# Stick-breaking attention pipelined over head pairs, and a pooling mixer with a root for its first tile alone

## The chip, the cores and the metric

The kernel runs on one core of one Trainium2 chip. The metric is the device time of one execution in microseconds (us), lower is better. Engines are named as the profile names them: PE is the matrix engine (TensorE), DVE is VectorE, ACT is ScalarE, POOL is GpSimd, SP is the engine whose queue issues most transfers. Every engine takes its instructions in the order in which they stand in its own queue and waits at the first one that isn't ready.

## The reference

A trunk of two layers over 512 tokens and 16 meta tokens (528 columns), width 1024. Each layer adds a token mixer and then a SwiGLU network to the residual h. Layer 0 mixes by causal pooling over four window lengths, layer 1 by stick-breaking attention with 16 heads of 64.

```python
def pool_mixer(h, w, scale):          # h is normalised with rmsnorm before
    ...
        outs.append((cs - lag) / cnt - xg)          # window mean minus the token, per group of 256
    pooled = jnp.stack(outs, axis=2).astype(h.dtype)
    mixed = jnp.einsum('blgc,gcd->blgd', pooled, w).reshape(B, L, D_MODEL)
    return mixed * scale

def _sb_attend(qs, qpos, kvs, kpos):
    ...
    z = jnp.einsum('bqhd,bkhd->bhqk', q, k).astype(jnp.float32) * (HEAD_DIM ** -0.5)
    log_keep = jnp.where(mask, jax.nn.log_sigmoid(-z), 0.0)
    later = lax.cumsum(log_keep, axis=3, reverse=True) - log_keep
    a = jnp.where(mask, jnp.exp(jax.nn.log_sigmoid(z) + later), 0.0)
    return jnp.einsum('bhqk,bkhd->bqhd', a.astype(v.dtype), v)
```

After the attention come `@ w_o`, the second SwiGLU network and a last rmsnorm.

## The kernel before

The residual is held transposed, as eight tiles `h0` to `h7` of 128 channels by 528 tokens. Every product is done as three products of a high and a low part: `wsplit` (L82) turns a loaded weight tile into `whi` on ACT (L92) and `wlo` on DVE (L97), and `mm3` (L102) issues the three matmuls per 128 rows (L106). A full weight tile of 1024 columns gives two such splits; the text calls one of them a W.

The order in which instructions stand in each engine's queue is set by a scheduler when the program is built, from the order of the code, from the buffers that are free and from explicit edges (`tc.issue_after(x)`: what the block holds stands behind x on x's engine). On the chip that order is fixed.

Start. Four token tiles x0 to x3 and the meta tile are loaded, their sums of squares are taken (ACT and DVE), `rstd_of` makes the inverse root (one ACT operation and three small DVE ones) for the tiles 0, 4 (meta) and 1 together and then for 2 and 3, and each tile is scaled and split into `ah` (ACT, L224) and `al` (DVE, L225). 30 matmuls on a zero tile (`warm`) run meanwhile. Pooling is a product with a band matrix, first for the left half of the 528 columns over all eight chunks, then for the right half. The mixing product (`mix`, L106, then the DVE addition L265) also runs over all chunks of the left half before the right one; `norm.chunk(c)` (L147) then makes the next network's operands `f0uh`, `f0ul` and the running sum of squares `f0sq` for chunk c.

Attention. The heads come in eight pairs. For a pair p, `proj(p)` has five steps: q (24 matmuls of 512 columns), and each half of k and of v (24 matmuls of 264 columns each). `scores` makes z in three groups of two PSUM banks each (832, 0, 416), and ACT takes two sigmoids of each group, into `kp` and `sg`. `weights(hd)` is, for each of the two heads, a scan over `kp` on DVE (L576) and a product into `sg` (L578). `turned(p, hd)` transposes `sg` on PE into two PSUM tiles `t1` and `t2` (ten transposes and one of `am`, ACT copies of sg's meta columns), which ACT copies into `a1`, `a2` (high parts) and DVE subtracts (low parts, L611) and corrects (`a0`, L614). `attend(p, hd)` multiplies by the values (`po`, nine matmuls), and `finish` splits the pair's output (`os`). `values` transposes v into `pv` and splits it into `vv`. `wo(p0, p1)` is the output product for the pairs p0 to p1-1, in eight steps, one for each chunk of h.

In iteration p of the loop the scores of pair p are issued first, then its values and steps of `proj(p + 1)` as filling, then `turned`, `attend` for both heads. The PSUM tag "two" (z, t1, pv) has two buffers of two banks, the tag "one" (pj, t2, po, pw) four of one bank.

Of the kernel before, what the change touches and what calls it, by code (L numbers as in the profile page):

```python
# [35 lines left out]
WARM = 30  # L36
# [14 lines left out]
def trunk(ctx: ExitStack, tc: tile.TileContext, x, meta, x_t, gain, pool_w, w_qkv, w_o, w_gate, w_up, w_down,  # L51
# [50 lines left out]
    def mm3(outs, wh, wl, xh, xl, start, stop, more=False):  # L102

        for i, (w, xx) in enumerate(((wh, xh), (wh, xl), (wl, xh))):
            for o, sl in outs:
                nc.tensor.matmul(o, lhsT=w, rhs=xx[:, sl], start=start and i == 0, stop=stop and i == 2,  # L106
                                 skip_group_check=more)
# [34 lines left out]


# [35 lines left out]
    with tc.tile_pool(name="start", bufs=1) as sp, phase("ps0", one=8):  # L179
# [11 lines left out]
        nc.sync.dma_start(out=band_raw, in_=c_band)  # L191
        nc.sync.dma_start(out=mband, in_=c_mband)
# [14 lines left out]
        for part in ((0, 4, 1), (2, 3)):  # L207
            i0 = part[0]
            n = len(part)
            ss = sp.tile([P, 3], F32, name=f"ss{i0}")[:, :n]  # L210
            nc.vector.memset(ss, 1.0)
            for j, i in enumerate(part):
                src, acc = (mt, ss[:META, j:j + 1]) if i == 4 else (xt[i], ss[:, j:j + 1])
                if i in (0, 2):
                    nc.scalar.activation(junk[0], src, AF.Square, accum_out=acc)
                else:
                    nc.vector.scalar_tensor_tensor(junk[1][:src.shape[0]], src, 1.0, src, op0=ALU.mult, op1=ALU.mult,
                                                   accum_out=acc)
            nc.vector.tensor_scalar(ss, ss, D * EPS, None, op0=ALU.add)
            r = rstd_of([(ss, slice(0, n))], *[sp.tile([P, 3], F32, name=f"rx{i0}{k}")[:, :n] for k in "rt"])  # L220
            for j, i in enumerate(part):
                rx[i] = r[:, j:j + 1]
        for i in range(4):
            nc.scalar.activation(ah[i], xt[i], AF.Copy, scale=rx[i])  # L224
            nc.vector.scalar_tensor_tensor(al[i], xt[i], rx[i], f32(ah[i]), op0=ALU.mult, op1=ALU.subtract)  # L225
            if i == 1:
                nc.scalar.activation(am[:META], mt, AF.Copy, scale=rx[4][:META])
        nc.vector.tensor_copy(band[:, :, BOFF:BOFF + 144], band_raw)
# [11 lines left out]
        for hf, terms in enumerate((((0, -META), (1, -144)), ((1, 120), (2, HALF - 272), (3, -136)))):  # L240
            for c in range(KC):
                g = c // 2
                cs = slice(c * P, (c + 1) * P)
                pp = ps(f"pool{c}{hf}", "one")[:, :HALF]
                for j, (i, off) in enumerate(terms):
                    rhs = band[:, g, BOFF + off:BOFF + off + HALF]
                    nc.tensor.matmul(pp, lhsT=ah[i][:, cs], rhs=rhs, start=j == 0, stop=False)
                    nc.tensor.matmul(pp, lhsT=al[i][:, cs], rhs=rhs, start=False, stop=j == len(terms) - 1)
                    if hf == 0 and j == 0:
                        nc.tensor.matmul(pp[:, 0:32], lhsT=am[:, cs], rhs=mband[:, g, :], start=False, stop=False)  # L250
                gc = gains[:, c:c + 1]
                a, b = ph[c][:, HV[hf]], pl[c][:, HV[hf]]
                nc.scalar.activation(a, pp, AF.Copy, scale=gc)
                nc.vector.scalar_tensor_tensor(b, pp, gc, f32(a), op0=ALU.mult, op1=ALU.subtract)
        pws = [wsplit(pwr[k], f"pw{k}") for k in range(2)]
        for hf in range(2):
            for c in range(KC):
                g, d = c // 2, c % 2
                pm = ps(f"mix{c}{hf}", "one")[:, :HALF]
                for k in range(2):  # L260
                    ds = slice(d * P, (d + 1) * P)
                    mm3([(pm, HV[hf])], pws[k][0][g][:, ds], pws[k][1][g][:, ds], ph[2 * g + k], pl[2 * g + k],
                        k == 0, k == 1)
                hv = hT[c][:, HV[hf]]
                nc.vector.scalar_tensor_tensor(hv, pm, gains[:, 32 + c:33 + c], hv, op0=ALU.mult, op1=ALU.add)  # L265
                if hf:
                    norm.chunk(c)


    def ffn(layer, gcol, norm, after):  # L270
# [67 lines left out]
        with tc.tile_pool(name=f"ffn{layer}", bufs=1) as fp:  # L338
# [13 lines left out]
            def plain(f):  # L352
                parts = [wsplit(raw_gu(kind, f), f"w{kind}{f}") for kind in ("gate", "up")]
# [131 lines left out]
    with tc.tile_pool(name="att", bufs=1) as ap, phase("ps2", one=4, two=2):  # L485
# [12 lines left out]
        def proj(p):  # L498

            got = {}  # L500
            first = {}

            def half(i, hf):
                if hf == 0:
                    got["w"] = wsplit(wraw(w_qkv[i * KC + p], f"r{'qkv'[i]}{p}"), f"w{'qkv'[i]}{p}")
                    got[i] = blk(f"qf{p}_{i}")
                wh, wl = got["w"]
# [3 lines left out]
                if p == 0:  # L511
                    if hf == 0:
                        first[i] = ps(f"pj{p}_{i}", "two", 2)
                    pj = first[i][:, hf, :n]
                else:
                    pj = ps(f"pj{p}_{i}{hf}", "one")[:, :n]
                for k in range(KC):
                    mm3([(pj, sl)], wh[k], wl[k], uh[k], ul[k], k == 0, k == KC - 1)
# [6 lines left out]
                if i == 0 or (i == 1 and hf == 1):  # L525
                    got["qk"[i]] = parts_of(p, i, f[:, TOK] if i == 0 else f)

# [23 lines left out]
        def scores(p, q, k):  # L551


            (qh, ql), (kh, kl) = q, k
            sg, kp = (ap.tile([P, 2, STRIP], F32, tag=t, name=f"{t}{p}", bufs=1) for t in ("sg", "kp"))

            for o, n, regs in ((832, 512, ((3, 0, META, L),)), (0, 416, ((0, 0, 0, 144), (1, 144, 0, 272))),
                               (416, 416, ((2, 0, 0, 400), (3, 400, 0, META)))):
                tz = ps(f"z{p}_{o}", "two", 2)
# [7 lines left out]
                for d in DIAG:  # L567
                    if o <= d < o + n:
                        for hd in range(2):
                            nc.tensor.matmul(tz[:, hd, d - o:d - o + P], lhsT=masks[:, 2], rhs=masks[:, 0], start=False,  # L570
                                             stop=True, skip_group_check=True)
                for dst, sc in ((kp, -1.0), (sg, 1.0)):
                    nc.scalar.activation(dst[:, :, o:o + n], tz[:, :, 0:n], AF.Sigmoid, scale=sc)  # L573

            def weights(hd):
# [5 lines left out]
            with tc.issue_after(weights(0)):  # L581
                weights(1)
            return sg[:, 0], sg[:, 1]
# [52 lines left out]
        def finish(p, of):  # L636
            a, b = (ap.tile([P, SEQ], F32R, tag="os", name=f"os{p}{n}", bufs=11) for n in "hl")
# [4 lines left out]
        def wo(p0, p1):  # L642
# [4 lines left out]
            def step(c):  # L647
# [5 lines left out]
                for j in range(n):  # L653
                    mm3([(pj, slice(0, SEQ))], wh[j], wl[j], *osp[p0 + j], j == 0, j == n - 1)
                nc.vector.tensor_tensor(out=hT[c][:, TOK], in0=pj, in1=hT[c][:, TOK], op=ALU.add)

            return [lambda c=c: step(c) for c in range(KC)]

        NP = NH // 2
        got, steps, values = proj(0)  # L660
        for st in steps:
            st()
        early = wo(0, 2)
        for p in range(NP):
            of = ap.tile([P, SEQ], F32, tag="of", name=f"of{p}", bufs=1)
            extra = []
            if p < NP - 1:
                nxt, nsteps, nvalues = proj(p + 1)
                before = []
                fill = nsteps[0:1], nsteps[1:2], nsteps[2:3], nsteps[3:4], nsteps[4:]  # L670
                if p == NP - 2:
                    late, fill = nsteps[3:], fill[:3] + ([], [])
                if 3 <= p < NP - 1:
                    extra = early[:4] if p == NP - 2 else early[:2 if p == 3 else 1]
                    early = early[len(extra):]
            else:
                w = wo(2, 4)
                before, fill = late, (w[0:1], w[1:2], w[2:3], w[3:4], w[4:5])
            with tc.issue_after(last) if p else nullcontext():
                s0, s1 = scores(p, got["q"], got["k"])  # L680
            for st in before:
                st()
            values()
            for st in list(fill[0]) + list(fill[1]):
                st()
            w0 = turned(p, 0, s0)
            for st in fill[2]:
                st()
            attend(p, 0, w0, got["v"], of)
            w1 = turned(p, 1, s1)  # L690
            for st in fill[3]:
                st()
            last = attend(p, 1, w1, got["v"], of)
            finish(p, of)
            for st in list(fill[4]) + list(extra):
                st()
            got, values = nxt, nvalues
# [83 lines left out]
```

## Time and profile before

| | us |
|---|---|
| median of 3 runs (lowest, highest) | 1086.45 (1085.02, 1087.53) |
| the profiled execution's own time | 1087.54 |
| its span in the profile | 1085.6 |
| PE busy | 1030.8 (95%) |
| DVE busy | 856.2 (79%) |
| ACT busy | 558.2 (51%) |

The stages, by the first matmuls in the trace: the start until 40.6, the first SwiGLU network until 410.4, attention with its output product until 723.4, the second network and the last norm until the end. A share of the span is a mean over these stages. An instruction's duration is longer than the distance to the next one on the same engine, since neighbours overlap: a matmul of 264 columns is shown as 0.28 and the next one starts 0.12 later. Sums are therefore made from starts.

### The profile page before, as it was taken

To read this page: it belongs to the slowest core of one execution; us is meant where nothing else is said; L and a number is where in the kernel's file an instruction comes from. 1 tells how busy PE (TensorE), PEld (TensorE's weight loads), DVE (VectorE), ACT (ScalarE), POOL (GpSimd) and SP (SyncE) were. 2 spreads that over 40 slices of the span, in tenths; PEclk is the share of its full clock that TensorE was granted. 3 is DMA by queue.
4 is the path that set the end of the run, shared out by engine and by line. 5 is a ranking of instruction groups with operands and counts; after the bars stand their busy time and mean duration, and the time that the engine had idled before them with its cause. 6 is when DMAs were issued, how large, how long until landed. Compare 5 with 4: busy or idle time off the path is not lost.

```text
span 1085.6 us, 18620 instructions
## 1 busy us (share of the span) xinstructions
PE 1030.8 (95%) x7302; PEld 956.6 (88%) x7302; DVE 856.2 (79%) x1529; ACT 558.2 (51%) x1131; POOL 6.2 (1%) x16
## 2 busy tenths in 40 slices
PE   8998999999999999798888899799999999999997
PEld 6997999999999998787788778678899999999985
DVE  7899987878888685766688768789987777878855
ACT  7555644545444454555554545356664454455544
POOL 1000000000000010000000000000000000000000
PEclk9999999999999999899999999899999999999999
DMA  9112332233232332101110102222233232333312
GB/s 346 65 53 73 133 98 98 98 98 98 98 97 98 117 108 88 39 30 40 49 59 21 49 30 79 78 97 69 77 105 101 98 98 97 108 107 117 98 39 78
DMA packets 43111, 95.72 MB, mean 88 GB/s; under 512 B 3328, under 2 KB 20096, under 8 KB 43024
## 3 DMA queue, kind: packets, MB, share of 16 engines
q1 hardware_dynamic: 42272, 93.40, 25.9%
q8 instruction: 57, 0.93, 0.3%
q10 hardware_dynamic: 752, 1.14, 0.3%
q14 instruction: 30, 0.25, 0.1%
HBM read 92.43 MB, written 2.10 MB: 87 GB/s over the span
## 4 chain that ended last, share of the span: by engine, by line
PE 80%; DVE 15%; ACT 2%; issue 1%; DMA 1%; SPq 0%; ACTq 0%; DVEq 0%
PE pb L106 15%; PE pd L106 11%; PE pd L330 11%; PE pj L106 11%; PE pa L106 10%; PE pc L106 10%; DVE kp L576 3%; PE pw L106 2%; PE po L628 2%; PE pp L106 2%; PE z L564 2%; PE t L589 2%; DVE sg L578 1%; DVE xl L389 1%; ACT kp L573 1%
## 5 line engine op out<-in xcount | busy, mean ns | idle before, releaser
L576 DVE TENSOR_TENSOR_SCAN kp<-kp,estrip 128x1344 f32<-128x1344 f32 x16 | 47.3, 2954 | 21.0 <-ACT kp L573 21.0
L303 DVE TENSOR_TENSOR h<-pd,h 128x264 f32<-128x264 f32 x96 | 41.2, 431 | 13.9 <-PE pd L106 13.9
L92 ACT CAST ws_3h<-rgate 128x512 fp32r<-128x512 f32 x38 | 23.6, 621 | 55.3 <-PE pb L106 49.3
L589 PE MATMUL t<-consts,sg 128*128 128x128 f32 x160 | 26.1, 319 | 25.5 <-DVE sg L578 22.4
L92 ACT CAST ws_5h<-s 128x512 fp32r<-128x512 f32 x38 | 23.6, 621 | 47.0 <-PE pb L106 36.3
L589 PEld LDWEIGHTS t<-consts,sg 128*128 128x128 f32 x160 | 21.7, 163 | 28.1 <-issue 24.2
L106 PE MATMUL pa<-xl,ws_0h 128*128 128x264 f32 (+1 forms) x152 | 43.4, 285 | 3.2 <-DVE xl L389 3.2
L432 DVE TENSOR_TENSOR u<-pb,m 128x264 f32<-128x264 f32 (+1 forms) x38 | 16.3, 430 | 38.1 <-PE pb L106 38.0
L92 ACT CAST ws_4h<-s 128x512 fp32r<-128x512 f32 x38 | 23.6, 621 | 42.3 <-PE pa L106 25.6
L106 PE MATMUL pb<-xl,ws_1h 128*128 128x264 f32 (+1 forms) x152 | 43.1, 284 | 1.0 <-DVE xl L389 1.0
L106 PE MATMUL pc<-xh,ws_2l 128*128 128x264 f32 (+1 forms) x152 | 43.2, 284 | 0.0
L106 PE MATMUL pb<-xh,ws_1h 128*128 128x264 f32 (+1 forms) x152 | 43.2, 285 | 0.0
L106 PE MATMUL pa<-xh,ws_3h 128*128 128x264 f32 (+1 forms) x152 | 43.1, 284 | 0.0
L106 PE MATMUL pa<-xh,ws_0l 128*128 128x264 f32 (+1 forms) x152 | 43.1, 284 | 0.0
L106 PE MATMUL pb<-xh,ws_6l 128*128 128x264 f32 (+1 forms) x152 | 43.1, 283 | 0.0
L106 PE MATMUL pa<-xl,ws_3h 128*128 128x264 f32 (+1 forms) x152 | 43.0, 283 | 0.0
L106 PE MATMUL pb<-xh,ws_4l 128*128 128x264 f32 (+1 forms) x152 | 43.0, 283 | 0.0
L106 PE MATMUL pc<-xl,ws_2h 128*128 128x264 f32 (+1 forms) x152 | 43.0, 283 | 0.0
L106 PE MATMUL pc<-xl,ws_5h 128*128 128x264 f32 (+1 forms) x152 | 43.0, 283 | 0.0
L106 PE MATMUL pb<-xl,ws_6h 128*128 128x264 f32 (+1 forms) x152 | 43.0, 283 | 0.0
L106 PE MATMUL pc<-xh,ws_2h 128*128 128x264 f32 (+1 forms) x152 | 43.0, 283 | 0.0
L106 PE MATMUL pb<-xl,ws_4h 128*128 128x264 f32 (+1 forms) x152 | 43.0, 283 | 0.0
(1179 smaller groups left out, 4177.6 us busy)
## 6 DMA issues: line engine op xcount, KB each, us to landing
rgate<-in_ffn_w_gate_dram SPq DMA_DIRECT2D x44, 512.0 KB, 3.5
rup<-in_ffn_w_up_dram SPq DMA_DIRECT2D x44, 512.0 KB, 3.4
rd<-in_ffn_w_down_dram SPq DMA_DIRECT2D x42, 512.0 KB, 3.6
rq<-in_sb_w_qkv_dram SPq DMA_DIRECT2D x8, 512.0 KB, 3.4
rk<-in_sb_w_qkv_dram SPq DMA_DIRECT2D x8, 512.0 KB, 3.4
rv<-in_sb_w_qkv_dram SPq DMA_DIRECT2D x8, 512.0 KB, 3.5
h<-in_x_t_dram SPq DMA_DIRECT2D x8, 264.0 KB, 6.8
x<-in_x_dram SPq DMA_DIRECT2D x4, 512.0 KB, 5.4
```

Source lines behind the costliest of these rows:

```text
L92: nc.scalar.copy(hi, v[:, j:j + w])
L106: nc.tensor.matmul(o, lhsT=w, rhs=xx[:, sl], start=start and i == 0, stop=stop and i == 2, skip_group_check=more)
L303: nc.vector.tensor_tensor(out=hv, in0=pd, in1=hv, op=ALU.add)
L330: nc.tensor.matmul(pd, lhsT=hid[j][x_][:, ts], rhs=w_[:, sl], start=r > 0 and i + j == 0, stop=j == len(hid) - 1 and i == 2, skip_group_ch ...
L389: nc.vector.tensor_tensor(out=xl[i][:, m, :], in0=o, in1=f32(xh[i][:, m, :]), op=ALU.subtract)
L432: tt(out=u[:, a], in0=pb, in1=m1, op=ALU.add)
L564: nc.tensor.matmul(tz[:, hd, c:c + k1 - k0], lhsT=qq[hs, i * P:(i + 1) * P], rhs=kk[hs, k0:k1], start=j == 0 and c == 0, stop=False, skip_ ...
L573: nc.scalar.activation(dst[:, :, o:o + n], tz[:, :, 0:n], AF.Sigmoid, scale=sc)
L576: nc.vector.tensor_tensor_scan(kp[:, hd, ::-1], kp[:, hd, ::-1], estrip[:, ::-1], 1.0, op0=ALU.mult, op1=ALU.max)
L578: return nc.vector.tensor_tensor(out=sg[:, hd, 0:STRIP - 1], in0=sg[:, hd, 0:STRIP - 1], in1=kp[:, hd, 1:STRIP], op=ALU.mult).ins
L589: nc.tensor.transpose(o, sg[:, c0:c0 + n], ident)
L628: last = nc.tensor.matmul(po[:, i0 * P:512], lhsT=lw, rhs=a, start=t == 0 and j == 0, stop=t == 4)
```

## The change

Start: x0 is loaded in two halves on the queues of SP and ACT; the band matrices are loaded on ACT's queue; x0's square is taken by ACT and DVE, half each, and `roots` makes its inverse root alone, then one for tile 1 and meta, then one for 2 and 3. The order of ACT and DVE there is written by hand (`tc.manual_schedule`), with the copy of the band matrix ahead of the first root on DVE. 18 `warm` matmuls instead of 30. Pooling of the left half issues tile 0's products for all chunks first. The mixing product runs chunk by chunk, both halves of a chunk, and `norm.chunk(c)` follows each chunk. The splits of `pool_w` are queued behind the last `split`, those of the first gate and up weights behind chunk 5's pooled halves (`norm.after`).

Attention: `scores` becomes a class with one call for each group, and `begin` issues the three groups of the next pair with steps of `proj` between them, inside the iteration of the pair before: after `turned(p, 1)` and ahead of `attend(p, 1)`. A pair's steps are spread over two iterations (k, k, q in the one, both halves of v in the next). The output product's steps are grouped 0 to 1, 2 to 4 and 5 to 7 instead of 0 to 1, 2 to 3 and 4 to 7: the first group's eight steps are issued in the iterations 4 and 5, the second's in 6 and 7, the third's at the end. `os` has 10 buffers instead of 11.

```diff
-WARM = 30
+WARM = 18
...
-        nc.sync.dma_start(out=xt[0], in_=x[0, 0:P, :])
         nc.scalar.dma_start(out=mt, in_=meta)
+        for h, q in zip(HD2, (nc.sync, nc.scalar)):
+            q.dma_start(out=xt[0][:, h], in_=x[0, 0:P, h])
         nc.sync.dma_start(out=xt[1], in_=x[0, P:2 * P, :])
+        nc.scalar.dma_start(out=band_raw, in_=c_band)
+        nc.scalar.dma_start(out=mband, in_=c_mband)
         nc.scalar.dma_start(out=gains, in_=gain)
...
+        for a in (ah, al):
             for c in range(KC):
+                pool(c, pps[c], 0, -META, (a,), start=a is ah)
...
-        for hf in range(2):
-            for c in range(KC):
-                g, d = c // 2, c % 2
+        for c in range(KC):
+            g, d = c // 2, c % 2
+            for hf in range(2):
                 pm = ps(f"mix{c}{hf}", "one")[:, :HALF]
...
-                if hf:
-                    norm.chunk(c)
+            norm.chunk(c)
...
-            a, b = (ap.tile([P, SEQ], F32R, tag="os", name=f"os{p}{n}", bufs=11) for n in "hl")
+            a, b = (ap.tile([P, SEQ], F32R, tag="os", name=f"os{p}{n}", bufs=10) for n in "hl")
...
+        def begin(p, got, before, between):
+            sc = Scores(p, got["q"], got["k"])
+            mark = None
+            for st in before:
+                mark = st()
+            with tc.issue_after(mark) if mark else nullcontext():
+                sc.group(0)
+                mark = sc.group(1)
+            for st in between:
+                with tc.issue_after(mark):
+                    mark = st()
+            with tc.issue_after(mark):
+                sc.group(2)
+            sc.both()
+            return sc.sg
...
+        sg = begin(0, got, [], steps[3:4])
+        steps[4]()
+        values()
+        nxt, steps, values = proj(1)
+        for st in steps[:3]:
+            st()
+        early, w = wo(0, 2), wo(2, 5)
         for p in range(NP):
...
+            w0 = turned(p, 0, sg[:, 0])
+            for st in steps[3:] if p + 1 < NP else w[4:6]:
+                st()
+            if p + 1 < NP:
+                values()
+            attend(p, 0, w0, v, of)
+            w1 = turned(p, 1, sg[:, 1])
+            got = nxt
+            if p + 2 < NP:
+                nxt, steps, values = proj(p + 2)
+                fill = steps[1:2], steps[2:3], steps[0:1]
+            elif p + 2 == NP:
+                fill = w[0:1], w[1:2], w[2:4]
             else:
+                fill = [], [], w[6:8]
+            if p + 1 < NP:
+                sg = begin(p + 1, got, fill[0], fill[1])
+            for st in fill[2]:
+                st()
+            attend(p, 1, w1, v, of)
+            if p in (4, 5):
+                for st in early[4 * (p - 4):4 * (p - 3)]:
+                    st()
             finish(p, of)
         norms[1] = Norm(24, "f1")
-        for c, st in enumerate(wo(4, NP)):
-            if c < 3:
-                w[5 + c]()
+        for c, st in enumerate(wo(5, NP)):
             st()
             norms[1].chunk(c)
```

What it makes of the queues is shown at three places; rows that repeat a row above them for another part of the same product are left out.

PE before, in iteration 4, from the third score group of pair 4 (`z4_416`) to the transposes of its first head (`t140`). `pv4` is the pair's values, `pj5_00` and `pj5_10` are q and the first half of k of pair 5:

```order
L564 MATMUL z4_416_7047<-qk4_1h_6860,qk4_0h_6762 128x400 x2
L570 MATMUL z4_416_7047<-masks_63 128x128
L539 MATMUL pv4_7068<-consts_61,qf4_2_6918 128x128 x4
L106 MATMUL pj5_00_7090<-anuh7_5466,wq5h4_7085 128x512
L106 MATMUL pj5_10_7131<-anuh0_5188,wk5h0_7122 128x264
L589 MATMUL t140_7161<-consts_61,sg4_7015 128x128 x8
```

PE now, from the same group through both heads' transposes to the first score group of pair 5 (`z5_832`). `po31` is the product with the values of pair 3's second head, `pj5_20` v of pair 5:

```order
L615 MATMUL z4_416_7089<-qk4_1h_6757,qk4_0h_6819 128x400 x2
L106 MATMUL pj5_00_7121<-anuh0_5194,wq5h0_7112 128x512
L681 MATMUL po31_7151<-a131h_6976,vv3_6615 128x512
L642 MATMUL t140_7173<-consts_61,sg4_6990 128x128 x8
L106 MATMUL pj5_20_7211<-anuh0_5194,wv5h0_7202 128x264
L681 MATMUL po40_7274<-a140h_7186,vv4_6943 128x512
L642 MATMUL t241_7292<-consts_61,sg4_6990 128x128 x2
L642 MATMUL t141_7291<-consts_61,sg4_6990 128x128 x8
L106 MATMUL pj6_10_7331<-anuh0_5194,wk6h0_7322 128x264
L615 MATMUL z5_832_7357<-qk5_1h_7085,qk5_0h_7147 128x512 x2
```

Between a pair's last score group and its transposes there now stand all of q of the next pair and the other pair's `po`, where three matmuls of q and one half of k stood.

DVE before, from the scan of pair 4's first head (`kp4`) to the product of its second (`sg4`):

```order
L576 SCALAR_TENSOR_TENSOR kp4_7016<-kp4_7016,estrip_5480 128x1344
L524 TENSOR_TENSOR qf5_0_7089<-pj5_00_7090,r8_5541 128x512
L546 TENSOR_TENSOR vv4_7076<-pv4_7068,vv4_7076 128x10x64
L578 TENSOR_TENSOR sg4_7015<-sg4_7015,kp4_7016 128x1343
L97 TENSOR_TENSOR wk6l0_7465<-rk6_7462,wk6h0_7464 128x512
L532 TENSOR_TENSOR qk5_0l_7117<-qf5_0_7089,qk5_0h_7116 128x512
L524 TENSOR_TENSOR qf5_1_7130<-pj5_10_7131,abr_5533 128x264
```

DVE now, from the scan of pair 3's first head to the rows that pair 4's score groups wait for: `a131l` frees the PSUM tile that `z4_832` takes, `vv4` the one that the second group takes. Left out are the same kinds of rows again: the second scan and product, three W, two `qf`, the second `of`, `a231l` and its `a0`:

```order
L629 SCALAR_TENSOR_TENSOR kp3_6663<-kp3_6663,estrip_5486 128x1344
L631 TENSOR_TENSOR sg3_6662<-sg3_6662,kp3_6663 128x1343
L97 TENSOR_TENSOR wv5l0_7203<-rv5_7200,wv5h0_7202 128x512
L567 TENSOR_TENSOR qf4_0_6792<-pj4_00_6793,r8_5547 128x512
L684 TENSOR_TENSOR of2_6512<-po21_6823,sh21_6833 64x512
L576 TENSOR_TENSOR qk4_0l_6820<-qf4_0_6792,qk4_0h_6819 128x512
L664 TENSOR_TENSOR a130l_6859<-t130_6845,a130h_6858 128x1024
L664 TENSOR_TENSOR a230l_6861<-t230_6846,a230h_6860 128x256
L667 SCALAR_TENSOR_TENSOR a0_5494<-a0h30_6862,consts_61,t230_6846 32x128 x4
L692 TENSOR_TENSOR os2l_6837<-of2_6512,os2h_6836 128x512
L664 TENSOR_TENSOR a131l_6977<-t131_6963,a131h_6976 128x1024
L590 TENSOR_TENSOR vv4_6943<-pv4_6935,vv4_6943 128x10x64
```

Nothing stands any longer between the first head's scan and its product; the scores of the next pair now wait at the end of this queue, behind all DVE work on the pair before.

DVE now, at the program's start:

```order
L216 SCALAR_TENSOR_TENSOR junk1_125,ss0_126<-x0_82 128x512
L245 CAST band_112<-bandr_87 128x4x144
L225 SCALAR_TENSOR_TENSOR ss0_126<-ss0_126 128x1
L136 TENSOR_TENSOR rx0t_138<-rx0r_137 128x1
L138 SCALAR_TENSOR_TENSOR rx0t_138<-ss0_126,rx0t_138 128x1
L139 SCALAR_TENSOR_TENSOR rx0r_137<-rx0t_138,rx0r_137 128x1
L216 SCALAR_TENSOR_TENSOR junk1_125,ss1_127<-x1_83 128x512
L235 SCALAR_TENSOR_TENSOR al0_118<-x0_82,rx0r_137,ah0_114 128x512 x2
```

Before, the squares of the meta tile and of x1 stood ahead of the first root, and the band copy just ahead of `al0`; now the root of x0 comes ahead of x1, and the band copy ahead of the root.

More of the change, by code (lines that the diff above doesn't have):

```diff
@@ L206, in trunk, with square @@
         rx = {}
[L207 to L220, printed above, removed]
+        def square(eng, src, acc):
+            out = junk[eng][:src.shape[0], :src.shape[1]]
+            if eng:
+                nc.vector.scalar_tensor_tensor(out, src, 1.0, src, op0=ALU.mult, op1=ALU.mult, accum_out=acc)
+            else:
+                nc.scalar.activation(out, src, AF.Square, accum_out=acc)
@@ L222, in trunk, with split @@
                 rx[i] = r[:, j:j + 1]
[L223 to L228, printed above, removed]
+        def split(i, h):
+            a = nc.scalar.activation(ah[i][:, h], xt[i][:, h], AF.Copy, scale=rx[i])
+            b = nc.vector.scalar_tensor_tensor(al[i][:, h], xt[i][:, h], rx[i], f32(ah[i][:, h]), op0=ALU.mult,
+                                               op1=ALU.subtract)
+            return a.ins, b.ins
@@ new lines, in trunk @@
+        pps = [ps(f"pool{c}0", "one")[:, :HALF] for c in range(KC)]
+        for a in (ah, al):
+            for c in range(KC):
+                pool(c, pps[c], 0, -META, (a,), start=a is ah)
+        for c in range(KC):
+            nc.tensor.matmul(pps[c][:, 0:32], lhsT=am[:, c * P:(c + 1) * P], rhs=mband[:, c // 2, :], start=False,
+                             stop=False)
+            pool(c, pps[c], 1, -144, (ah, al), stop=True)
+            pooled(c, 0, pps[c])
+        for c in range(KC):
+            pp = ps(f"pool{c}1", "one")[:, :HALF]
+            for j, (i, off) in enumerate(((1, 120), (2, HALF - 272), (3, -136))):
+                for a in (ah, al):
+                    pool(c, pp, i, off, (a,), start=j == 0 and a is ah, stop=j == 2)
+            done = pooled(c, 1, pp)
+            if c == 5:
+                norm.after = done
@@ L259, in trunk @@
+        with tc.issue_after(split_done[0]), tc.issue_after(split_done[1]):
+            pws = [wsplit(pwr[k], f"pw{k}") for k in range(2)]
+        for c in range(KC):
+            g, d = c // 2, c % 2
+            for hf in range(2):
                 pm = ps(f"mix{c}{hf}", "one")[:, :HALF]
@@ L352, in plain @@
             def plain(f):
-                parts = [wsplit(raw_gu(kind, f), f"w{kind}{f}") for kind in ("gate", "up")]
+                with ExitStack() as order:
+                    for ins in norm.after if f == 0 else ():
+                        order.enter_context(tc.issue_after(ins))
+                    parts = [wsplit(raw_gu(kind, f), f"w{kind}{f}") for kind in ("gate", "up")]
                 g, sg, u = (gw(f"{i}{f}") for i in ("g", "sg", "u"))
@@ L660, in trunk @@
         got, steps, values = proj(0)
-        for st in steps:
+        for st in steps[:3]:
             st()
-        early = wo(0, 2)
+        sg = begin(0, got, [], steps[3:4])
+        steps[4]()
+        values()
+        nxt, steps, values = proj(1)
+        for st in steps[:3]:
+            st()
+        early, w = wo(0, 2), wo(2, 5)
         for p in range(NP):
             of = ap.tile([P, SEQ], F32, tag="of", name=f"of{p}", bufs=1)
[L666 to L675, printed above, removed]
-            else:
[L677 to L686, printed above, removed]
```

123 lines of the change are left out of this document (72 added, 51 removed).

## The prediction

> **What bounds the kernel now.** I read the page's busy shares first, then the chain that ended last, then the waits, and then each stage by windows.
>
> ```profile
> PE 1030.8 (95%) x7302; PEld 956.6 (88%) x7302; DVE 856.2 (79%) x1529; ACT 558.2 (51%) x1131; POOL 6.2 (1%) x16
> PE t L589 <- DVE sg L578: 22.4, 8, 5.3
> 410.40:723.40 313.00, 279.23 (x1820) 244.37 (x1820) 230.32 (x330) 154.64 (x308) 0.00 (x0) 0.95 0.17 54
> 474.29:506.63 32.34, 28.86 (x205) 26.02 (x204) 24.07 (x33) 16.36 (x34) 0.00 (x0) 0.95 0.15 50
> 506.63:538.98 32.35, 27.49 (x205) 24.40 (x204) 23.63 (x34) 16.13 (x34) 0.00 (x0) 1.00 0.13 42
> 671.13:696.76 25.63, 20.08 (x109) 17.16 (x108) 22.86 (x32) 10.21 (x26) 0.00 (x0) 0.87 0.15 50
> ```
>
> The second row is one of the waits: PE waited 22.4 us, eight times, at a pair's transposes for DVE's product into `sg`. The others are windows (stretch, its length, then busy PE, PEld, DVE, ACT, POOL, the granted clock, DMA). PE is full in the two networks, but in attention (410.4 to 723.4) it idles 313.0 - 279.2 = 33.8 us, and at a mean clock of 0.95 loses some 15 more. Two pairs, from scan to scan, take 32.34 and 32.35 us, though one lost clock and the other none: DVE's chain sets this period, not PE. The chain behind the wait:
>
> ```profile
> 572.90 0.28 PE L570 MATMUL z<-masks 128*128 128x128 bf16 x2
> 573.02 0.61 PE L539 MATMUL pv<-consts,qf 128*128 128x128 f32 x4
> 573.22 0.86 ACT L573 ACTIVATE kp<-z 128x832 f32<-128x832 f32 x1 [2.88 <-PE z L570]
> 574.12 2.96 DVE L576 TENSOR_TENSOR_SCAN kp<-kp,estrip 128x1344 f32<-128x1344 f32 x1 [3.05 <-ACT kp L573]
> 577.58 0.81 DVE L546 TENSOR_TENSOR vv<-pv,vv 128x640 fp32r<-128x640 f32 x1
> 578.31 1.55 DVE L578 TENSOR_TENSOR sg<-sg,kp 128x1343 f32<-128x1343 f32 x1
> 580.00 2.37 PE L589 MATMUL t<-consts,sg 128*128 128x128 f32 x10 [2.63 <-DVE sg L578]
> 480.00:484.00 4.00, 3.83 (x21) 3.86 (x22) 4.00 (x5) 1.58 (x5) 0.00 (x0) 0.60 0.00 0
> 510.00:514.00 4.00, 1.49 (x13) 1.52 (x14) 4.00 (x4) 1.58 (x6) 0.00 (x0) 1.00 0.01 4
> ```
>
> Scores end at 573.1, the scan starts 1.0 later, the product ends at 579.86, and PE has run out of work at 577.4. After such a gap the clock is often halved (0.60 over 480 to 484, so 1.6 us lost), though not always (1.00 over 510 to 514).
>
> **The change, part by part: the pairs.** The score groups move ahead by most of a pair. Between the last group and the transposes PE now has q of the next pair and one `po`. PE's prices:
>
> ```profile
> 585.91 1.25 PE L589 MATMUL t<-consts,sg 128*128 128x128 f32 x10
> 589.70 2.93 PE pj L106 x24
> 592.63 1.51 PE po L628 x9
> 598.40 0.50 PE L564 MATMUL z<-qk_1h,qk_0h 64*128 64x512 f32 x2
> 599.51 0.51 PE L564 MATMUL z<-qk_1h,qk_0h 64*128 64x144 f32 x4
> 600.63 0.48 PE L106 MATMUL pj<-anuh,wq6h 128*128 128x512 f32 x1
> 600.82 4.91 PE pj L106 x21
> ```
>
> A half of k or v is 2.93, q 24 x 4.91/21 = 5.61, a `po` 1.51, transposes 1.25, the score groups 1.11 and 1.12 (from start to start) and 1.10, `pv` 0.6 (573.02 on). After the last score group the product is ready in 1.0 + 2.9 + 1.5 = 5.4 us, as `qf` and `vv` no longer stand between; PE has 5.61 + 1.51 = 7.1 us of work. The wait of 2.6 goes.
>
> A pair's PE work without output product is 4 x 2.93 + 5.61 + 2 x 1.51 + 2 x 1.25 + 3.33 + 0.6 = 26.8 us. What is late next is DVE. The next pair's first score group needs the PSUM tile that `a1l` of the second head frees, at the end of DVE's queue. Before, DVE worked without a pause from the scan to the start of `qk_1l`:
>
> ```profile
> 574.12:593.09 18.97, 15.45 (x108) 14.77 (x107) 18.73 (x25) 8.85 (x22) 0.00 (x0) 0.91 0.05 16
> 589.53 0.68 DVE L97 TENSOR_TENSOR wv6l<-rv,wv6h 128x512 fp32r<-128x512 f32 x1
> 593.83 0.68 DVE L631 TENSOR_TENSOR of<-po,sh 64x512 f32<-64x512 f32 x1
> 596.78 0.69 DVE L639 TENSOR_TENSOR os4l<-of,os4h 128x512 fp32r<-128x512 f32 x1
> ```
>
> The new stretch holds the same operations, and one W, two `of` and one `os` more, and `vv` less: 0.68 + 2 x 0.68 + 0.69 - 0.81, less about 0.08 overlap for each of three, is 1.7. So 18.97 + 1.7 = 20.7 us from scan to `a1l`. Behind it come 0.1 of handover, two groups 2.23, half of k 2.93, the third group 1.10, and 1.0 to the next scan: 28.0. ACT has a W and `qk_1h` ahead of the last sigmoid, which I put at 0.3. The period is then 28.3, with PE idle some 1.5 in gaps below 1 us, which I price at full clock.
>
> The first pair: q ends at 410.40 + 5.6 = 416.0, the norm's two matmuls at 416.7, k at 422.6. The root's chain:
>
> ```profile
> 418.91 0.68 ACT L134 ACTIVATE abr<-abp 128x264 f32<-128x264 f32 x2
> 419.62 0.71 DVE L135 TENSOR_TENSOR abt<-abr 128x528 f32<-128x528 f32 x1 [1.30 <-ACT abr L134]
> 422.38 0.69 DVE L524 TENSOR_TENSOR qf<-pj,r 128x512 f32<-128x512 f32 x1
> ```
>
> ACT can end `abr` at 418.6 (two W, a table load of 1.28, `abr`); 2.8 of DVE follow (419.62 to 422.38), and seven operations of `qf`, W and the splits, 3.7, until q and k are split at 425. Scores so wait 1.9 at 422.6, which is new. Two groups, v and the third group end at 431.5, and the first scan starts at 432.5 (before 442.64). PE goes on with v, `pv`, q and k of pair 1 to 446.3, transposes, v, `po`, transposes, `pv`, k (13.4) to 459.7, scores with half of k to 466.0: scan of pair 1 at 467.0, before 474.29.
>
> Four periods of 28.3 lead to 580.2 for pair 5. Each of the next two carries four steps of the output product, 24 x 0.234 = 5.6, which DVE's slack covers: 26.8 + 5.6 = 32.4, to 612.6; in the other, 21 + 9 matmuls of the second output group replace k (30 x 0.234 - 5.86 = +1.2) and the wait of some 0.3 comes back: 33.9, to 646.5. Before, pair 7's scan was at 671.13.
>
> Tail. From z's end at 645.5 PE has 6 matmuls and a `po`, 2.9, and then waits for the product, which ends at 6.6 since an addition and a W (1.2) stand between scan and product: 3.7 idle, and 1.6 of halved clock behind it. Then transposes, 18 matmuls, `po`, transposes, 18 matmuls, `po`: 13.9, to 22.1; and 72 matmuls of the last output group, 16.8. The last pair's `os` is ready after 24 of these that don't need it. End at 645.5 + 39.0 = 684.5; before 723.4: **-38.9**. `os` with ten buffers makes pair 5's wait for the first output group, which stands ahead of it anyway: 0.
>
> The second network. DVE has 32 operations of some 0.63 between the first result of the last group (29.3 behind 645.5) and the sum of squares, so the norm's matmuls come at 49.4, 10.4 behind the last product. Before:
>
> ```profile
> 732.66 1.06 PE L172 MATMUL fb1p<-f1sq,ones 128*128 128x264 f32 x4
> ```
>
> 9.3 behind it. That is 1.1 lost, but six matmuls (1.4) more are done by then. Bounds -1 and +3; I take **+0.5**.
>
> **The start.** Rows:
>
> ```profile
> 9.96 0.46 DVE L228 CAST band<-bandr 128x576 fp32r<-128x576 f32 x1
> 10.56 1.09 PE L247 MATMUL pool<-band,ah 128*128 128x264 f32 x7
> 40.59 0.78 PE L106 MATMUL pp<-f0uh,wgate0h 128*128 128x264 f32 x2 [2.19 <-DVE h L265]
> 49.45 0.71 DVE L127 SCALAR_TENSOR_TENSOR f0sq<-f0sq,f0sq 128x528 f32<-128x528 f32 x1
> 54.50 0.71 DVE L135 TENSOR_TENSOR fb0t<-fb0r 128x528 f32<-128x528 f32 x1 [2.15 <-ACT fb0r L134]
> ```
>
> The first pooling product moves from 10.56 to about 9 (root of x0 alone, the band copy at about 7 since its load is asked for 1 us earlier and past two tiles), but the last tile's `al` hardly moves: it hangs on the roots in a row. Fewer `warm` matmuls cost nothing: PE waits there either way. Pooling of the right half waits for PSUM that DVE frees after the splits of `pool_w`, as before. Chunk by chunk, `f0uh` and `f0ul` begin some 2 us earlier, the gap of 2.19 goes, and the sum of squares (49.45) comes within 1 us of where it was; but its matmuls no longer stand behind nearly all of the first gate and up products, so the root (54.50) moves to about 51. Between -1 (PE alone) and -4 (the root, on which DVE's full queue hangs): **-3**.
>
> **Sum.** -38.9 + 0.5 - 3 = -41.4 against the profiled execution's 1087.54: 1046.1. That execution is 1.1 above the median of 1086.45; **1046**, own range 1040 to 1053.
>
> **Rivals.** (A) The new gaps, though short, keep halving the clock. For it:
>
> ```profile
> 18.18 0.39 PE L248 MATMUL pool<-band,al 128*128 128x264 f32 x1 [0.93 <-DVE al L225]
> 20.00:23.00 3.00, 3.00 (x15) 3.00 (x15) 3.00 (x8) 2.81 (x7) 0.00 (x0) 0.51 1.04 414
> ```
>
> A gap of 0.93 (and one of 0.69 after it) led to 0.51 for 3 us; against it, 2.64 at 510 led to nothing. At 1.6 for each of seven pairs: +11, 1057. The Trainium skill, "TensorE: Matmul & The Clock Gate" (Part 1), says the gate falls back after an idle window of about 3.4 us. By that rule A could not be and the sum stays; the trace disagrees, as gaps of 2.63 halved it, so A keeps its chance.
>
> (B) DVE keeps ahead and PE is the bound: period 26.8, 4 x 1.5 and some 2 elsewhere less: 1038. For it, DVE idles a quarter of the old period; against it, the 20.7 have no gap.
>
> (C) The change doesn't do what it says: the transposes still wait, because ACT or DVE start a pair's chain over 1.7 us late (7.1 - 5.4). Then the periods stay near 32, and only prologue, tail and start gain, 7.3 + 14 + 3: 1063.
>
> (D) Slower: a W whose load is late now blocks DVE's queue ahead of `a1l`, and with it the next pair's scores; every us is paid in full. It decides from 41/6 = 7 us a pair; at 8, 1094. Against it: DMA is busy 0.13 to 0.17 of these stretches, and loads are asked for as buffers come free, a pair ahead.
>
> **Chances.** Forecast 0.62, A 0.18, B 0.08, C 0.06, D 0.03, other 0.03. The range takes in the forecast and A's and B's times: 1038 to 1060. About 0.2% (2.2 us) is what a measurement of this kernel can tell from no change: faster 0.95, same 0.01, slower 0.04.
>
> **What would show it.** Scan to scan of one pair at 28.3 and no wait of PE at the transposes for `sg` except in the last pair (about 3.7); PE's wait at the first score group for `a1l` below 1 us; the first scan near 429 and the end of the output product near 682 (with the start's 3 us); the granted clock at 0.98 or more from pair 1 to 6; the first network's root near 51. I am wrong if the transposes wait for `sg`, if scores wait several us for DVE, or if the clock stays at 0.95.

## The result, and the profile after

| us | before | changed kernel |
|---|---|---|
| median, lowest to highest | 1085.94 (1085.02 to 1087.53), 4 runs | 1065.53 (1064.88 to 1067.63), 4 runs |
| profiled execution: time, span | 1087.54, 1085.6 | 1065.42, 1063.6 |

The ratio is 0.9816, 95% interval 0.9804 to 0.9829: 20.4 us faster where 41.4 were forecast, and outside the range. The busy shares, the waits of PE, then windows: attention with its output product, a pair, the last two pairs' periods, and the tail from the last pair's first scan.

```profile
PE 1021.2 (96%) x7290; PEld 950.1 (89%) x7290; DVE 856.2 (80%) x1535; ACT 560.1 (53%) x1138; POOL 6.2 (1%) x16
PE pp L106 <- DVE h L708: 4.1, 1, 4.1
PE t L642 <- DVE sg L631: 3.6, 1, 3.6
PE pp L106 <- ACT f0sq L159: 3.6, 1, 3.6
PE pool L275 <- ACT ah L234: 2.7, 1, 2.7
PE z L615 <- DVE a121l L664: 0.5, 1, 0.5
412.85:693.02 280.17, 268.07 (x1820) 234.70 (x1820) 225.27 (x322) 150.79 (x303) 0.00 (x0) 0.99 0.18 59
469.95:498.93 28.98, 27.78 (x206) 24.69 (x205) 24.27 (x34) 16.38 (x34) 0.00 (x0) 1.00 0.17 55
585.16:619.15 33.99, 32.98 (x229) 28.91 (x228) 28.12 (x42) 17.60 (x38) 0.00 (x0) 1.00 0.19 59
619.15:654.36 35.21, 34.02 (x210) 28.24 (x209) 28.77 (x42) 17.56 (x38) 0.00 (x0) 1.00 0.24 79
654.36:693.02 38.66, 35.07 (x160) 28.95 (x158) 32.80 (x47) 19.28 (x41) 0.00 (x0) 0.91 0.20 69
```

The eight waits for `sg`, 22.4 us in all, are one of 3.6, in the last pair; a pair takes 28.98 instead of 32.35; the clock is 1.00 through the pairs. But three waits of PE, all outside the pairs, are new or longer: 2.7 at the first pooling product (before: none), 3.6 and 4.1 at the first product of each network (before: 2.2 and 0.9).

Stage by stage in the two profiled executions (the stages end at the first q product, at the start of the last output matmul, and at the end of the span):

| stage | before | after | change | forecast |
|---|---|---|---|---|
| start and first network | 410.4 | 412.85 | +2.4 | -3 |
| attention | 312.6 | 279.9 | -32.6 | -38.9 |
| second network | 362.6 | 370.8 | +8.2 | +0.5 |
| sum | 1085.6 | 1063.6 | -22.0 | -41.4 |

The start, in time's order on PE, DVE and ACT:

```profile
1.34 6.66 PE L265 MATMUL warm<-warm 128*128 128x512 bf16 x18 [1.34 <-DVE warm L262]
10.74 2.13 PE L275 MATMUL pool<-band,ah 128*128 128x264 f32 x8 [2.75 <-ACT ah L234]
15.56 0.63 PE L289 MATMUL pool<-mband,am 128*128 128x32 f32 x2 [0.93 <-ACT am L256]
30.50 0.28 PE L106 MATMUL mix<-ph,pw0h 128*128 128x264 f32 x1
45.96 0.48 PE L106 MATMUL pp<-f0uh,wgate0h 128*128 128x264 f32 x2 [3.58 <-ACT f0sq L159]
8.59 0.46 DVE L245 CAST band<-bandr 128x576 fp32r<-128x576 f32 x1 [1.81 <-DMA bandr<-in_c_band_dram]
9.15 0.20 ACT L135 ACTIVATE rx0r<-ss 128x1 f32<-128x1 f32 x1 [2.69 <-DVE ss L225]
20.14 1.28 DVE L97 TENSOR_TENSOR pw0l<-pwr,pw0h 128x512 fp32r<-128x512 f32 x2
45.34 0.48 DVE L312 SCALAR_TENSOR_TENSOR h<-mix,gains,h 128x264 f32<-128x264 f32 x1
10.74:27.06 16.32, 15.39 (x69) 15.08 (x70) 13.94 (x31) 12.97 (x25) 0.00 (x0) 0.50 0.97 364
```

The band's load landed at 8.5, and the root's sum stood behind the copy that waits for it, so ACT waited 2.69. `warm` ended at 8.0, and after the gap of 2.75 all pooling ran at clock 0.50 until 27.06. Mixing began at 30.5 (before: 26.5). The last addition to h, 45.34 (before: 39.95), releases the first gate product. The row names ACT's square, which ended just as late, but the gate product doesn't read it; a later run with the same wait (3.59) names the addition.

The second network, DVE and then PE:

```profile
683.46 1.29 DVE L708 TENSOR_TENSOR h<-pw,h 128x512 f32<-128x512 f32 x2 [4.29 <-PE pw L106]
696.50 0.68 DVE L708 TENSOR_TENSOR h<-pw,h 128x512 f32<-128x512 f32 x1
703.66 0.70 DVE L128 SCALAR_TENSOR_TENSOR f1sq<-f1sq,f1sq 128x528 f32<-128x528 f32 x1
692.79 0.40 PE L106 MATMUL pw<-os7h,wo_7l 128*128 128x512 f32 x1
697.33 0.76 PE L106 MATMUL pp<-f1uh,wgate0h 128*128 128x512 f32 x1 [4.14 <-DVE h L708]
709.71 1.05 PE L175 MATMUL fb1p<-f1sq,ones 128*128 128x264 f32 x4
697.33:700.33 3.00, 3.00 (x7) 2.42 (x8) 3.00 (x5) 1.16 (x2) 0.00 (x0) 0.50 0.51 156
```

The last output product is done at 693.0, but its addition to h begins at 696.50, behind weights' low parts and the norm's operations in DVE's queue. The first gate product waits 4.14 for it, and PE then runs at half clock. In the profile before, the same wait was this:

```profile
724.25 0.47 PE L106 MATMUL pp<-f1uh,wgate0h 128*128 128x512 f32 x1 [0.90 <-DVE h L655]
```

The norm's matmuls (`fb1p`, which add the sum of squares over the channels) come 16.9 behind the last output matmul's start (before: 732.66 - 722.96 = 9.7). They don't wait for the sum of squares, which ended at 704.4: they stand in PE's queue behind 42 gate and up matmuls (before: 36, and the sum of squares ended at 728.1).

### The profile page after: what moved, and what is told of

Read it like the earlier page. It is cut to its first block, busy times and chain, and to the rows that moved or that the text cites. A ratio compares the mean times of both kernels' runs of the same rounds, so it can differ in the third digit from the quotient of the medians.

```text
span 1063.6 us, 18572 instructions
## 1 busy us (share of the span) xinstructions
PE 1021.2 (96%) x7290; PEld 950.1 (89%) x7290; DVE 856.2 (80%) x1535; ACT 560.1 (53%) x1138; POOL 6.2 (1%) x16
## 4 chain that ended last, share of the span: by engine, by line
PE 80%; DVE 15%; ACT 2%; issue 2%; DMA 1%; ACTq 0%; DVEq 0%
PE pb L106 15%; PE pd L106 12%; PE pd L376 11%; PE pc L106 10%; PE pa L106 10%; PE pj L106 8%; PE pp L106 4%; DVE kp L629 2%; PE pw L106 2%; PE z L615 2%; PE pool L275 1%; PE mix L106 1%; DVE xl L438 1%; DVE a L667 1%; PE t L642 1%
## 5 line engine op out<-in xcount | busy, mean ns | idle before, releaser
L92 ACT CAST ws_3h<-rgate 128x512 fp32r<-128x512 f32 x38 | 23.6, 621 | 55.2 <-PE pb L106 49.1
L481 DVE TENSOR_TENSOR u<-pb,m 128x264 f32<-128x264 f32 (+1 forms) x38 | 16.3, 428 | 40.2 <-PE pb L106 40.2
L106 PE MATMUL pb<-xh,ws_4h 128*128 128x264 f32 (+1 forms) x152 | 42.9, 282 | 0.9 <-ACT m L460 0.9
L106 PE MATMUL pa<-xh,ws_0h 128*128 128x264 f32 (+1 forms) x152 | 43.1, 284 | 0.0
L106 PE MATMUL pc<-xh,ws_5h 128*128 128x264 f32 (+1 forms) x152 | 42.9, 282 | 0.0
```

The lines of the kernel that those rows point to most:

```text
L92: nc.scalar.copy(hi, v[:, j:j + w])
L106: last = nc.tensor.matmul(o, lhsT=w, rhs=xx[:, sl], start=start and i == 0, stop=stop and i == 2, skip_group_check=more)
L481: tt(out=u[:, a], in0=pb, in1=m1, op=ALU.add)
```

## The experiments

The kernels were timed beside the kernel before, in three sets; ratios are to it. It took 1085.2, 1086.3 and 1086.4 in them, so times of different sets can differ by 1.2 for that alone, and their ratios are the better comparison. "Attention alone" is the changed kernel with the old start.

**The start.** First the clock alone, and the whole old start.

```diff
-WARM = 18
+WARM = 30
```

> The changed kernel with 30 warm matmuls instead of 18, nothing else. In the changed kernel PE stood still from 8.0 to 10.74 and then ran all pooling at half clock until 27.06. Theory 'DVE sets the start': DVE works from 20.1 to the last addition to h at 45.8 with only 1.6 us of waits for PE's and ACT's pooled halves, so the clock is worth at most those 1.6: first gate product at 44.3 (45.96), attention from 411.2 (412.85), time 1063.9 against 1065.5. Rival 'the clock sets it': the mixing product starts where it did before, at 26.5 instead of 30.5, and everything behind it comes 4 us earlier: attention from 408.9, time 1061.5. Second rival: the next wait of PE, 0.9 us at 14.6, halves the clock again, and nothing changes by more than 0.5.

1064.02 (ratio 0.9798, 0.9781 to 0.9814). Mixing began at 28.5 (30.5), attention at 412.1. DVE's theory gave the time, though attention began 0.9 later than it says; the clock returned only 2.0 of 4, since PE, now faster, waits 2.47 for the meta tile and halves again (0.73 on the mean from there to the mixing). The two intervals overlap, so the 1.5 us is likely rather than shown; the 2.0 at the mixing is in the trace.

> The changed kernel with the start of the kernel before (loads, roots, splits, pooling, mixing, 30 warm matmuls); attention as changed. Theory: the new start costs what the trace shows, 412.85 - 410.40 = 2.45 us at the start of attention, and the parts add up: attention from 410.4, time 1063.1 against 1065.5. Rival, as predicted: the new start is worth -3 and the loss lies elsewhere in the first network: attention at 413 or later, time 1065.5 to 1068.5.

1059.11 (0.9756, 0.9740 to 0.9772), 6.4 less than the changed kernel, and the intervals are apart. Mixing at 25.0, the root at 51.5, attention at 408.0. The new start is a loss, larger than the 2.4 of the stage table: before's profiled execution had lost clock from 18.2 to 23.3 (0.68) and behind the first gate product (0.50 over 3 us), this one had not (1.00 in both). Not all of the difference is the start: of the 7.1 between the two profiled executions 4.9 is there when attention begins, and 2.9 comes behind the last output product, where the wait of 4.1 is the same; attention takes 0.7 from the sum. Next, only the mixing's order of the new start:

```diff
-        for hf in range(2):
-            for c in range(KC):
+        for c in range(KC):
+            for hf in range(2):
 ...
-                if hf:
-                    norm.chunk(c)
+            norm.chunk(c)
```

> The kernel with the old start and the changed attention (1059.1), and of the new start only the mixing product chunk by chunk, both halves of a chunk, each followed by the norm's part. It tells the loads, roots and splits from the order of the mixing. Theory: chunk by chunk is a gain by itself, as predicted (the norm's low parts begin 2 us earlier and the gap of 2.2 ahead of the first gate product goes): attention from 406 instead of 408.0, time 1057. What costs in the new start is then the rest, loads, roots and splits: 8. Rival 'DVE has no slack there': the last addition to h comes behind more of the norm's operations, the gap at the first gate product grows to 3.6 as in the changed kernel, and time is 1059 to 1061.

1060.10 (0.9762, 0.9745 to 0.9778): no gain in the time. The root came 26.4 behind the first mixing product (26.5 with the old order), and the gap at the first gate product was 2.5 instead of 2.2. But this execution had lost clock at the same two places as before's (0.70 from 18 to 23, 0.52 behind the first gate product), and before's root came 28.0 behind its first mixing product. From that product to attention it is 382.6 here, 383.9 before and 383.0 with the old start: at like clock the new order may be worth 1.3, which the times don't show. The loss lies ahead of the mixing, in loads, roots and splits. Two of them by themselves, first `pool_w`'s splits behind the last tile's split, in attention alone:

```diff
-        pws = [wsplit(pwr[k], f"pw{k}") for k in range(2)]
+        with tc.issue_after(done[0]), tc.issue_after(done[1]):
+            pws = [wsplit(pwr[k], f"pw{k}") for k in range(2)]
```

> The kernel with the old start and the changed attention (1059.1), and of the new start only that pool_w's splits stand behind the last tile's split instead of ahead of the second root. Theory 'DVE's queue is full behind the last split': four low parts, 2.5 us, now stand behind it, and the old cover (DVE waiting for ACT's high parts) gives back 0.8: mixing starts 1.7 later, attention from 409.7 instead of 408.0, time 1060.8. Rival 'the second root comes earlier by as much': 1059.1.

1064.18 (0.9793, 0.9772 to 0.9814; single runs 1061.3 to 1065.6), more than the theory's 1060.8. The profiled execution is the fastest of these, and what the others lost beyond it was not traced. In it mixing began at 27.4 instead of 25.0, attention at 410.2 instead of 408.0: the theory, with 2.4 where it gave 1.7. PE waits for the PSUM that DVE's pooled low parts free, now behind the splits, and the clock halves behind that wait:

```profile
19.95 0.59 PE L250 MATMUL pool<-band,ah 128*128 128x264 f32 x1 [3.15 <-DVE pl L257]
19.95:23.00 3.05, 3.05 (x14) 3.05 (x15) 3.05 (x8) 2.21 (x6) 0.00 (x0) 0.50 1.03 410
```

Then the band's copy, in the changed kernel with 30 `warm`:

```diff
-            nc.vector.tensor_copy(band[:, :, BOFF:BOFF + 144], band_raw)
             roots((0,), 2)
             square(0, xt[1][:, HD2[0]], sums[1][:, 0:1])
             square(1, xt[1][:, HD2[1]], sums[1][:, 2:3])
+            nc.vector.tensor_copy(band[:, :, BOFF:BOFF + 144], band_raw)
```

> The changed kernel with 30 warm matmuls (1064.0), and the copy of the band matrix on DVE behind the first root and the square of tile 1's half instead of ahead of the root. In the changed kernel DVE waits 1.81 for the band's load (landed at 8.5) with the root's sum queued behind it, and ACT 2.69 for that sum. Theory 'the band copy ahead of the root delays both roots': first root 1.9 earlier, the second and the meta tile's split (which PE waited 2.47 for) 1.5 to 1.9 earlier, mixing from 26.9 instead of 28.5, time 1062.2. Rival 'ACT is full': ACT has the squares of three tiles and the high parts in a row, the meta tile's split moves by less than 0.5, time 1064.0.

1062.03 (0.9781, 0.9764 to 0.9798), mixing at 26.94: the theory, to the tenth for the mixing. The interval overlaps that of the kernel it changes, so the gain in time is likely rather than shown; the 1.6 at the mixing is in the trace.

```profile
7.28 0.16 DVE L136 TENSOR_TENSOR rx0t<-rx0r 128x1 f32<-128x1 f32 x1 [0.27 <-ACT rx0r L135]
8.68 0.46 DVE L248 CAST band<-bandr 128x576 fp32r<-128x576 f32 x1 [0.24 <-DMA bandr<-in_c_band_dram]
13.88 0.41 PE L289 MATMUL pool<-mband,am 128*128 128x32 f32 x2 [1.65 <-ACT am L256]
```

The root comes 2.1 earlier (9.38 in the changed kernel), the copy waits 0.24 instead of 1.81, and the meta tile's products start at 13.9 instead of 15.7. At the first mixing product the three parts are worth 2.0 (`warm`), 1.6 (band) and 2.4 (splits), 6.0 in all, against 5.5 between the two starts. The third is a price in the old start: in the two kernels with the new start and 30 `warm`, PE waits for nothing between the meta tile's products and the mixing. There the clock was 0.73 and 0.74 on the mean in that stretch, so how much of the 1.9 that is left (26.94 against 25.01) is the splits' and how much the clock's stays open, and loads and roots by themselves were not tried. Behind the first mixing product nothing is lost: to attention it is 382.4 in the changed kernel.

**The second network.**

```diff
-        early, w = wo(0, 2), wo(2, 5)
+        early, w = wo(0, 2), wo(2, 4)
 ...
-        for c, st in enumerate(wo(5, NP)):
+        for c, st in enumerate(wo(4, NP)):
```

> The changed kernel with the output product grouped as before, pairs 0 to 1, 2 to 3, 4 to 7: the last group has 12 matmuls a chunk (2.8 us) instead of 9 (2.1). Theory 'the last group is too short for DVE': with 9 matmuls DVE falls behind (2.5 us a chunk for the addition, the low part, the square's sum and a weight's low part), the last addition to h comes 3.9 us after the last product, and the first gate product waits for it. With 12 the wait of 4.1 goes to about 0.9 and the half clock behind it (2.5 us) goes; the two last iterations lose 24 matmuls (-5.6) and the end gains them (+5.6), the wait for the last pair's product grows by 0.7: -5 in all, 1060.5. Rival 'DVE's own chain sets the root whatever PE does': the sum of squares ends 21 us of DVE work behind the first addition of the last group, which comes 4 us earlier: -4 at most, with the wait of 4.1 still there: 1061.5. Second rival: nothing is gained, since the matmuls only change places: 1065.5.

1067.03 (0.9822, 0.9805 to 0.9838): nothing gained, the second rival. The wait at the first gate product was 2.10, where the theory gave 0.9. The gate product came 2.0 sooner behind the last output matmul (2.5 instead of 4.5 from start to start), but of the 24 matmuls taken out of the last two iterations only 1.5 us came back (33.7 instead of 35.2 in one, none in the other): there they had filled waits of PE, and the end pays 5.4 of their 5.6 (43.8 instead of 38.4 from the last pair's scan to the last output matmul).

```diff
-                    for ins in norm.after if f == 0 else ():
+                    for ins in norm.after if f == 0 else (norm.end,) if f == 1 and layer in (1,) else ():
```

`norm.end` is the last addition to the sum of squares.

> The changed kernel, but in the second network the low parts of the second gate and up weights (four operations of DVE, 0.6 each) stand behind the sum of squares instead of among the last additions to h. Theory 'the first gate product waits for the last addition to h, which stands in DVE's queue behind such weights': three of the four move out from ahead of it, so the wait of 4.1 becomes 2.3 and the time is 1.8 less, 1063.7. Rival 'the root sets it': the sum of squares comes 3.0 earlier and all 3.0 are gained, 1062.5. Second rival: nothing, since the weights' low parts are then late for the second block: 1065.5.

1062.17 (0.9786, 0.9771 to 0.9800). The wait, ahead of the same product, is as expected (the row names ACT's square again, and the last addition to h ended 0.15 ahead of the product, as in the changed kernel):

```profile
696.56 0.47 PE L106 MATMUL pp<-f1uh,wgate0h 128*128 128x512 f32 x1 [2.30 <-ACT f1sq L159]
```

3.4 less than the changed kernel. 1.8 of it is this wait. The rest may be clock: this execution ran at 1.00 from the gate product to the norm's matmuls (43 matmuls in 10.0), the changed kernel's at 0.77 (42 in 12.4). A shorter wait doesn't always keep it: behind the 2.10 of the kernel above the clock was 0.72 over 3 us.

**The pairs.** In the changed kernel the chain of pair 2, from scan to scan:

```profile
498.93 2.96 DVE L629 TENSOR_TENSOR_SCAN kp<-kp,estrip 128x1344 f32<-128x1344 f32 x1
517.14 0.41 DVE L664 TENSOR_TENSOR a221l<-t,a221h 128x256 fp32r<-128x256 f32 x1
517.48 1.41 DVE L667 SCALAR_TENSOR_TENSOR a<-a0h,consts,t 32x128 fp32r<-32x128 f32 x4
518.92 1.22 DVE L664 TENSOR_TENSOR a121l<-t,a121h 128x1024 fp32r<-128x1024 f32 x1
520.06 0.81 DVE L590 TENSOR_TENSOR vv<-pv,vv 128x640 fp32r<-128x640 f32 x1
520.20 0.50 PE L615 MATMUL z<-qk_1h,qk_0h 64*128 64x512 f32 x2 [0.47 <-DVE a121l L664]
527.91 2.96 DVE L629 TENSOR_TENSOR_SCAN kp<-kp,estrip 128x1344 f32<-128x1344 f32 x1
```

`a1l` ends 21.1 behind the scan (forecast: 20.7), the next scan comes 7.85 later (forecast: 7.6). `a2l` and `a0`, 1.8 together, stand ahead of `a1l` though only the late `po` needs them. Two kernels change that; the edit is an edge (`low` is `a1l`'s subtraction, `ahead` that of `vv`, in the second kernel alone):

```diff
+            with tc.issue_after(low), tc.issue_after(ahead or low):
                 nc.vector.tensor_tensor(out=a2[1], in0=p2[:, 0:256], in1=f32(a2[0]), op=ALU.subtract)
 ...
                     nc.vector.scalar_tensor_tensor(a0[r, i], f32(a0h[r]), lo_rows[r], p2[r, 256:384], op0=ALU.mult,
```

> The changed kernel, but of a pair's second head the low part a1l stands on DVE ahead of a2l and a0 (1.75 us) instead of behind them; vv of the next pair stays behind all three. The period from scan to scan is 28.98 where 28.3 was predicted, and PE waits 0.3 to 0.6 at the first score group for a1l. Theory 'the chain runs through a1l alone': a1l ends about 1.4 earlier (its ACT copy ends at 517.5 in pair 2, the low part then at 518.65 instead of 520.06), and four periods and the last but one shorten by up to that: 27.6, time 1059.9. Rival 'vv is right behind it': the second score group takes the PSUM tile that vv frees, and vv ends at 520.8 whatever the order ahead of it: the wait of PE moves from the first to the second group (about 1 us each), the period stays at 29.0, and the time at 1065.5.

1064.59 (0.9805, 0.9788 to 0.9822), period 28.83: the rival. The wait moved to the second group:

```profile
PE z L615 <- DVE vv L590: 4.3, 7, 1.3
```

> As the kernel with a1l first, and vv of the next pair too stands ahead of a2l and a0 of the second head. Theory 'DVE's order ahead of the two PSUM tiles sets the period': both score groups come 1.4 earlier, period 27.6, and five periods bring -6: 1059.5. Rival 'PE is the bound by now': PE is busy 27.7 of 28.98 in a pair and keeps about 0.4 of gaps, so the period ends at 28.1: -4, 1061.5. Second rival 'the order doesn't matter': 1065.5.

1064.53 (0.9801, 0.9784 to 0.9817). The period is 28.42, and the first group waits for nothing:

```profile
518.72 1.23 DVE L663 TENSOR_TENSOR a121l<-t,a121h 128x1024 fp32r<-128x1024 f32 x1 [0.32 <-ACT a121h L662]
519.86 0.81 DVE L590 TENSOR_TENSOR vv<-pv,vv 128x640 fp32r<-128x640 f32 x1
520.82 0.50 PE L615 MATMUL z<-qk_1h,qk_0h 64*128 64x512 f32 x2
500.11:528.53 28.42, 27.66 (x205) 24.56 (x204) 24.36 (x33) 16.36 (x34) 0.00 (x0) 1.00 0.11 38
```

PE is the bound now, with 27.66 busy and 0.76 of small waits: the rival, at 28.4 instead of 28.1. From pair 1's scan to pair 7's it is 181.7 instead of 184.4; that 2.7 doesn't show apart from the scatter of the times, which alone would fit the second rival as well.

**All together**, a version that beats both kernels:

> Old start, changed attention, a1l and vv ahead of a2l and a0, and the low parts of the second gate and up weights behind the sum of squares in both networks. Theory: the parts add up: 1059.1 - 5 (pairs) - 2.5 (second network) - 1 (first network): 1050.5. Rival: with DVE relieved PE is the bound and a third of it is lost: 1054.

1054.46 (0.9708, 0.9692 to 0.9724): the rival's time, but not its reason. It is 11.1 below the changed kernel, and the single kernels' measured 6.4, 3.4 and 1.0 add to 10.8, so no third of them is lost; the theory had put the pairs at 5 where 1.0 was measured. The low parts in the first network, where the gap at the first gate product is 0.99, were not timed by themselves. The wait for `sg` in the last pair (3.6) and 2.3 at the second network's first product remain.

## Why the prediction was wrong, step by step

Of the 41.4 forecast, 19.4 are missing in the two profiled executions: 7.7 in the second network, 6.3 in attention and 5.4 in the start. (The sum was taken off the profiled execution; off the median it would have given 1045.)

- **The pairs: right in mechanism.** The transposes no longer wait, the next wait is `a1l` at the first score group at 0.3 to 0.6, and it appeared where it was said. First scan 22.5 behind the first q product (forecast 22.1), second pair's 34.6 later (34.5), the tail 38.7 to the end of the output product (38.0), with 3.6 of idle for the product (3.7). Rival A is out: the clock was 1.00 through the pairs, whose gaps were 0.6 at most. C and D did not happen, though C's time, 1063, is the nearest to the measured one: that is chance, as its periods near 32 did not come.
- **The period, 28.3: 28.98 three times, then 28.28.** The stretch to `a1l` was 0.4 short and what follows 0.2. Behind it lay a larger slip: the term "PE work per pair 26.8", a sum of starts over uniform runs of matmuls, is 27.7 busy in the trace, and with its small waits PE needs 28.4 once DVE is out of the way. So the forecast was itself at PE's bound, and rival B, with a period of 26.8, could not be. The same term made the two iterations with output product 32.4 and 33.9, where 34.0 and 35.2 came: 2.0 + 1.6 + 1.3 of the 6.3 lost here.
- **The start, -3: +2.4, and 4.9 against the old start at full clock.** Four sentences failed, and the root came at 55.2 where 51 was forecast. "Fewer `warm` matmuls cost nothing: PE waits there either way": the wait is free, the clock behind it is not. "The first pooling product moves to about 9, the band copy at about 7": the load landed at 8.5, and the copy that waits for it held DVE's queue ahead of the root, and so of the second root and the meta tile, on which every chunk's left half hangs; I had followed the first product and the last tile alone. "Pooling of the right half waits for PSUM that DVE frees after the splits of `pool_w`, as before": the splits now stand behind the last split, 2.5 us of a queue without a gap. In the old start that place cost 2.4; how much it cost in the new one isn't shown. "Chunk by chunk, ... the gap of 2.19 goes": it grew to 3.58, and to 2.53 where only the order was changed. That order, to which I gave the gain, brought nothing that the times show.
- **The second network, +0.5: +8.2.** The step that failed is "so the norm's matmuls come at 49.4": I counted DVE's 32 operations to the sum of squares, took the norm's matmuls to follow it, and let PE do gate products meanwhile. But those matmuls stand behind the gate products in PE's queue, before as well as now, and the first gate product waits for the last addition to h, one of these 32. It came 4.1 late instead of 0.9. That is 3.2; the clock of 0.50 behind it cost some 2.6, and six more matmuls ahead of the norm's 1.4; the last 1.0 came behind them and was not traced. The nearest row was in the profile before: the same wait, 0.90 at 724.25. The twelve matmuls a chunk that stood there gave DVE more time, though with twelve in the changed kernel the wait was still 2.10. Part of the 8.2 is scatter or another place of the norm's matmuls in PE's queue: from the last output product to the end it is 370.8 here, 367.9 to 369.8 in the seven other kernels with a wait of 4.1, and 362.6 before.

## What to carry to other kernels

When a stage gets shorter, look at the last instruction of every queue at its end: what is added up there decides when the next stage may begin, and work that had been hidden in the slower stage is in the way. A wait for a load costs what stands behind it in that queue, so here the copy of a constant belonged behind the first thing that the critical chain needed. And price the engine that will be the next bound from its busy time in a window, not from a sum of uniform pieces.

## What was not expected of the hardware

The gap of 2.75 at 8 us cost half the clock for 16.3 us, 11.5 of them without another gap. The same wait of 4.11 to 4.15 at the second network left a clock of 0.50 in the next 3 us of the changed kernel and 0.65 in attention alone. The two short gaps of the old start (0.93 and 0.69) halved the clock in one execution (0.68 on the mean from 18.2 to 23.3) and not in another (1.00). The Trainium skill, "TensorE: Matmul & The Clock Gate" (Part 1), has the clock fall after an idle window of about 3.4 us and come back after as long a busy one, with a free-running window; the scatter of like gaps fits that, the 16.3 us and the short gaps do not.
